# Up stage of a decoder layer: operands split in the order the products take them, bank copies with priority, norm broadcast later, two down tiles inside the last pair

## The chip, the cores and the metric

The kernel runs on one core of a Trainium2 chip, in one launch. The metric is the device time of one execution in microseconds. Three runs of the kernel before gave 1458.48, 1459.8 and 1460.78 us; the median is 1459.8 us.

## The reference

One decoder layer over 1024 positions of width 1024, in float32:

```python
h = h + hybrid_mixer(rmsnorm(h, norm_mix_g), ...)      # differential attention + conformer convolution
h = h + cross_attention(rmsnorm(h, norm_cross_g), rmsnorm(mem, norm_mem_g), w_cq, w_ckv, w_co)
h = h + conv_ffn(rmsnorm(h, norm_ffn_g), w_up, ffn_dw_w, w_down)
return rmsnorm(h, norm_final_g)

def conv_ffn(h, w_up, ffn_dw_w, w_down):
    up = jnp.einsum("bsd,df->bsf", h, w_up)            # 1024 -> 2 * 2816
    up = causal_dwconv(up, ffn_dw_w)                   # 3 taps along the sequence
    z = jax.nn.silu(up[..., :D_FF]) * up[..., D_FF:]
    return jnp.einsum("bsf,fd->bsd", z, w_down)        # 2816 -> 1024
```

The change lies in `conv_ffn`, in the last projection of the cross attention ahead of it and in the final norm behind it.

## The kernel before

Arrays stand with channels on the 128 partitions and the 1024 positions along the free dimension. A float32 product is made from three passes (`mm3`, lines 198 to 200): each operand is split into a rounded high part and the low rest, and hi*lo, lo*hi and hi*hi are added up in one PSUM bank of 128x512. A split (`split`) is a cast on ScalarE (line 220) and a subtraction on VectorE (line 221); weights of the other stages are split in `split_w` (lines 181 and 182).

The stages that matter here follow one another on TensorE.

*co*: the output projection of the cross attention, eight tiles `m`, each one `proj` of 48 matmuls into a two-bank tile `BIG`. For each half of a tile VectorE adds the residual to the bank (line 1220), the residual coming by a DMA that ScalarE's queue issues (line 1219) into a half-width buffer; ScalarE squares the sum for the norm (line 253), and VectorE adds the square to `acc` (line 254); ScalarE scales by the norm's gain into `x_` (line 1222); SyncE stores the whole tile to `h2_dr` (line 1223).

*up*: 22 pairs `p_` of a gate tile and a value tile. Both rows of weights, both halves of the 1024 input channels and both halves of the positions make a 2x2 by 2x2 block product, done with seven block products instead of eight (`product`, four k-tiles of three passes, 12 matmuls each). The weight operands are a11, a12, a22 and the sums q1 to q4 (`w_unit`; the sums are made by GpSimd, line 1191); the input operands are b11, b21, b22 and the differences n1, n2, t3, t4 (`unit`, in `late_sums` and in the loop over `m`). A pair runs as `prod1` (a11 with b11 into bank `b`; `b` copied out as p1, line 1291; a12 with b21 into bank `a`), `prod2` (q2 with n2 added to `b`; `b` copied as u2, line 1307; q3 with t3 into bank `c`; q1 with n1 added to `b`; `b` copied as u4, line 1312) and `prod3` (q4 with b22 added to `b`, a22 with t4 added to `c`). The three copies are on ScalarE and go into half-width buffers; the next product into `b` waits for them. After that come the taps of the depthwise convolution (line 1318 on ScalarE, line 1320 on VectorE), Silu on ScalarE (line 1331), and sums and products on VectorE (lines 1328, 1332, 1333, 1335); the result goes to `z_dr` (line 1336). The pair's order on TensorE is: `prod2(p)`, `prod1(p+1)`, `prod3(p)`; `prod1(0)` and `prod1(1)` come first. The inverse root mean square is found by `rf_stats` between them (16 small matmuls on line 1261, then a power on GpSimd, line 231) and spread over the partitions by `rf_bcast` (line 245) ahead of `prod2(0)`.

*down*: `z` is loaded back and split (`z_load`), the weights `dn` are split, and `down(c)` takes two of the 22 tiles at a time: for each of eight output tiles 12 matmuls into a `BIG`, which VectorE adds to the residual `h2` (line 1394). The last four tiles are in `final()`, with the norm and the output.

What sets the order: TensorE's order around the change is written out by hand (`tc.manual_schedule`). The order of the other queues (ScalarE, VectorE, GpSimd, SyncE) is fixed when the program is built, by a planner (`schedule_with_timeline_sim=True`, line 1559) that goes by readiness on its own estimate of time, and among ready instructions by priority; priority is the place in the program, and `tc.high_priority(offset=150)` puts an instruction 150 places forward. On the chip each queue is worked through in that fixed order.

Buffers that matter: 26 full-width buffers `t` (`R()`, `T()`), which hold the operands of the *co* stage (16 of them until its end) and then 26 of the input operands; 8 buffers `q` (`Q()`); 5 buffers `t2` (`T2()`) for the tiles of *co* and for weights and weight sums; 2 `whi` and 2 `wlo`, which `WU()` uses for weights by turns with `t2`; 3 buffers `raw`; 5 half-width buffers `half` (`halfT()`); eight PSUM banks `ub` (`UB()`) in *up*, which are the same banks as `BIG` and the others in *co* and *down*.

Of the kernel before, what the change touches and what calls it, by code (L numbers as in the profile page):

```python
# [10 lines left out]
F32R = mybir.dt.float32r  # L11
# [46 lines left out]
def hybrid_block_kernel(ctx: ExitStack, tc: tile.TileContext, xT, memT, pos, vecs, lams, ropec,  # L58
# [24 lines left out]
    def Q(dt=F32):  # L83
        return pq.tile([P, S], dt, tag="q", name=nm("q"))
# [16 lines left out]
    def halfT(dt=F32):  # L101
        return sm_.tile([P, HALF], dt, tag="half", name=nm("half"), bufs=5)
# [30 lines left out]
    def vcol(name, i=0):  # L133
        o, w = _COLS[name]
        return vec[:, o + i:o + i + 1]
# [66 lines left out]
    def hs(h):  # L202
        return slice(h * HALF, (h + 1) * HALF)
# [814 lines left out]
    def T2(dt=F32):  # L1018
        return p2.tile([P, S], dt, tag="t2", name=nm("t2"))
# [128 lines left out]
    late = []  # L1148

    def late_sums(j):  # L1150

        lo_, hi_ = xg[j], xg[4 + j]
        xb["b22"][j] = unit(hi_[:, hs(1)])
        nc.vector.scalar_tensor_tensor(out=lo_[:, hs(0)], in0=lo_[:, hs(0)], scalar=-1.0, in1=hi_[:, hs(1)],
                                       op0=ALU.mult, op1=ALU.subtract)
        xb["n2"][j] = unit(lo_[:, hs(0)])
        nc.vector.tensor_tensor(out=lo_[:, hs(1)], in0=hi_[:, hs(1)], in1=lo_[:, hs(1)], op=ALU.subtract)
        xb["t3"][j] = unit(lo_[:, hs(1)])
        nc.vector.scalar_tensor_tensor(out=hi_[:, hs(0)], in0=lo_[:, hs(0)], scalar=-1.0, in1=hi_[:, hs(0)],
                                       op0=ALU.mult, op1=ALU.subtract)  # L1160

    raws, wts, pairs = {}, {}, {}

    def w_load(p_):
# [10 lines left out]
    def WU():  # L1175

        tag = ("t2", "t2", "whi", "wlo", "t2", "whi", "wlo")[wcount[0] % 7]
        wcount[0] += 1
        return T2(F32R) if tag == "t2" else pw[0].tile([P, S], F32R, tag=tag, name=nm("wu"), bufs=2)

    def w_unit(name, p_):
        if p_ >= FT:
            return
        a, b = raws[p_]
        pr = pairs.setdefault(p_, {})

# [24 lines left out]
        wts[(name, p_)] = u  # L1211

    for m in range(8):
        ps = proj(need("co", m), xs_co) if m > 1 else co[m]
        hh = T2()
        x_ = Q()
        for half in range(2):
            res = halfT()
            nc.scalar.dma_start(out=res, in_=h_dr[m][:, hs(half)])
            nc.vector.tensor_tensor(out=hh[:, hs(half)], in0=ps[:, hs(half)], in1=res, op=ALU.add)  # L1220
            square_into(acc, hh[:, hs(half)], m == 0, hs(half))
            nc.scalar.mul(x_[:, hs(half)], hh[:, hs(half)], vcol("g_ffn", m))
        nc.sync.dma_start(out=h2_dr[m], in_=hh)
        xg.append(x_)
        if m == 6:
            w_load(0)
            for name in ("a11", "a12"):
                w_unit(name, 0)
        j = m % 4
        xb["b11" if m < 4 else "b21"][j] = unit(x_[:, hs(0)])  # L1230
        if m < 4:
            nc.vector.tensor_tensor(out=x_[:, hs(0)], in0=x_[:, hs(0)], in1=x_[:, hs(1)], op=ALU.subtract)
# [46 lines left out]
    def ev():  # L1279
        return halfT()  # L1280

    st = {}

    def prod1(p_):
        if p_ >= FT:
            return
        d = st[p_] = {}
        d["b"], d["a"] = UB(), UB()
        product(d["b"], "a11", p_, "b11", True)
        d["p1"] = ev()  # L1290
        nc.scalar.copy(out=d["p1"], in_=d["b"])
        product(d["a"], "a12", p_, "b21", True)

    def out1(p_):
# [8 lines left out]
    def prod2(p_):  # L1303
        d = st[p_]
        product(d["b"], "q2", p_, "n2", False)
        d["u2"] = ev()
        nc.scalar.copy(out=d["u2"], in_=d["b"])  # L1307
        d["c"] = UB()
        product(d["c"], "q3", p_, "t3", True)
        product(d["b"], "q1", p_, "n1", False)  # L1310
        d["u4"] = ev()
        nc.scalar.copy(out=d["u4"], in_=d["b"])
        d["uv"] = Q()
        nc.vector.tensor_tensor(out=d["uv"][:, hs(1)], in0=d["c"], in1=d["u4"], op=ALU.add)

# [22 lines left out]
    w_load(1)  # L1338
    with tc.manual_schedule(engines={mybir.EngineType.PE}):
        for name in ("a11", "a12"):  # L1340
            w_unit(name, 1)
        prod1(0)
        rf = rf_stats()
        for name in ("q2", "q3", "q1"):
            w_unit(name, 0)
        prod1(1)
        rf_bcast(rf)
        out1(0)
        for p_ in range(FT):
            w_unit("q4", p_)  # L1350
            w_unit("a22", p_)
            w_load(p_ + 2)
            prod2(p_)
            if p_ > 0:
                w_unit("a11", p_ + 1)
                w_unit("a12", p_ + 1)
                prod1(p_ + 1)
            out1(p_ + 1)
            for name in ("q2", "q3", "q1"):
                w_unit(name, p_ + 1)  # L1360
            prod3(p_)
    u_scope.close()


    big[0] = ctx.enter_context(tc.tile_pool(name="big2", bufs=2, space=PSUM, reuse_waits="tile"))
    bank[0] = ctx.enter_context(tc.tile_pool(name="bank3", bufs=4, space=PSUM, reuse_waits="tile"))
    wend[0] = len(seq)
    h2 = []
    for m in range(8):
        h2.append(Q())  # L1370
        nc.sync.dma_start(out=h2[m], in_=h2_dr[m])
    zt = {}
    zpos = [0]

# [6 lines left out]
            zt[zpos[0]] = (hi, lo)  # L1381
            zpos[0] += 1

    def down(c):
        ws = [need("dn", c, 1), need("dn", c + 1, 2)]
        z_load(c + 3)
        zs = [zt.pop(c), zt.pop(c + 1)]
        for m in range(8):
            ps = BIG()
            for i in range(2):  # L1390
                for h in range(2):
                    mm3(ps[:, hs(h)], (ws[i][0][:, bs(m)], ws[i][1][:, bs(m)]),
                        (zs[i][0][:, hs(h)], zs[i][1][:, hs(h)]), i == 0, i == 1)
            nc.vector.tensor_tensor(out=h2[m], in0=h2[m], in1=ps, op=ALU.add)  # L1394

    def final():
# [16 lines left out]
        def write(sl, rb):  # L1413
            w = sl.stop - sl.start
            g = S // w
            for m0 in range(0, 8, g):
                o = T()
# [19 lines left out]
        for m in range(8):  # L1437
            evac(m, banks[m], sl)

        gf = T()  # L1440
        nc.sync.dma_start(out=gf, in_=gfin.unsqueeze(0).to_broadcast([P, D]))
        hT = {}

        def residual(tb):
            hT[tb] = T()
# [12 lines left out]
            return ps  # L1458

        def finish(tb, ps):  # L1460
            h_, o = hT.pop(tb), T()
            ss = small(2, "fs", 2)
            for c in range(2):
                nc.vector.tensor_tensor(out=h_[:, hs(c)], in0=h_[:, hs(c)], in1=ps[c], op=ALU.add)
# [26 lines left out]
                residual(tb + 1)  # L1491
            finish(tb, ps)

    z_load(1)
    for c in range(0, FIN[0], 2):
        down(c)
    z_load(FT - 1)
    final()

# [63 lines left out]
```

## Time and profile before

| | |
|---|---|
| median of three runs | 1459.8 us |
| the profiled execution's own time | 1461.06 us |
| its span, first to last instruction | 1459.3 us |
| mean granted clock of TensorE | 0.988 of full speed |
| busy share of the span: TensorE, VectorE, ScalarE, GpSimd | 96%, 70%, 39%, 13% |
| *up*, from the last matmul of *co* to the first of *down* | 736.3 to 1194.2 us |

The span is what the profiler saw between the first and the last instruction; the execution's own time is 1.8 us longer, and 1.3 us above the median. A matmul of 512 columns is shown with 0.39 us, but in an unbroken row the next starts 0.23 us later: the starts tell the pace. "idle before <-releaser" names what ended the idle time of an engine ahead of an instruction.

### The profile page before, as it was taken

What the parts mean: (1) busy time and instruction counts of PE and PEld (TensorE: products, weight loads), DVE (VectorE), ACT (ScalarE), POOL (GpSimd) and SP (SyncE); (2) the same over time, 40 slices, a digit from 0 to 9 for tenths busy, and PEclk for the clock granted to TensorE, in tenths of its full rate; (3) what the DMA queues carried; (4) which work ended last, traced back from release to release, by engine and by line L of the source; (5) the groups of instructions that cost most, each with busy time, mean ns of one, the idle gap of its engine ahead of it and who ended that gap; (6) DMA issues with size and microseconds to landing.
All of it is one profiled execution on the core that took longest, in us unless ns stands there. A gap on an engine that the chain in (4) does not pass through costs nothing.

```text
span 1459.3 us, 17309 instructions
## 1 busy us (share of the span) xinstructions
PE 1407.3 (96%) x6709; PEld 1155.2 (79%) x6709; DVE 1026.5 (70%) x1375; ACT 573.3 (39%) x1015; POOL 193.7 (13%) x169
## 2 busy tenths in 40 slices
PE   9999999999999999999979999999999989999997
PEld 6888887777777888888867778778877867888886
DVE  7899998878855424454676787778787896666546
ACT  6211224677763323344453444434444451211103
POOL 0000000013110000000043322333332300000001
PEclk9999999999999999999989999999999999999999
DMA  6132225523405421103421222222222284323003
GB/s 225 40 94 65 70 82 148 175 85 87 116 15 194 166 80 58 58 30 115 137 87 57 73 87 73 76 83 87 73 87 73 85 326 166 105 69 101 15 1 116
DMA packets 44131, 141.54 MB, mean 97 GB/s; under 512 B 5776, under 2 KB 8080, under 8 KB 44048
## 3 DMA queue, kind: packets, MB, share of 16 engines
q1 hardware_dynamic: 37552, 123.65, 25.9%
q10 hardware_dynamic: 6496, 16.78, 3.6%
q8 instruction: 53, 0.87, 0.2%
q14 instruction: 30, 0.25, 0.1%
HBM read 101.51 MB, written 28.41 MB: 89 GB/s over the span
## 4 chain that ended last, share of the span: by engine, by line
PE 76%; DVE 9%; ACT 4%; issue 4%; DMA 4%; POOL 2%; SPq 0%; POOLq 0%; ACTq 0%; DVEq 0%
PE big L198 15%; PE big L199 15%; PE big L200 15%; PE ub L198 5%; PE ub L199 5%; PE ub L200 5%; DVE q L1320 2%; POOL t L1191 2%; PE big L703 2%; PE tb L772 2%; PE big L701 2%; DMA uraw<-in_wu_dram 2%; ACT q L1318 2%; PE bk L198 1%; PE bk L199 1%
## 5 line engine op out<-in xcount | busy, mean ns | idle before, releaser
L199 PE MATMUL big<-r,wlo 128*128 128x512 f32 x624 | 243.1, 390 | 0.6 <-DVE wlo L182 0.6
L200 PE MATMUL big<-r,whi 128*128 128x512 f32 x624 | 243.0, 389 | 0.0
L198 PE MATMUL big<-r,whi 128*128 128x512 f32 x560 | 219.1, 391 | 2.3 <-DVE r L304 1.2
L1394 DVE TENSOR_TENSOR q<-q,big 128x1024 f32<-128x1024 f32 x72 | 87.8, 1219 | 78.0 <-PE big L200 78.0
L181 ACT CAST whi<-raw 128x1024 fp32r<-128x1024 f32 x58 | 61.2, 1056 | 205.1 <-PE big L200 168.3
L1320 DVE SCALAR_TENSOR_TENSOR q<-q,vec,q 128x1023 f32<-128x1023 f32 x88 | 120.1, 1365 | 27.6 <-ACT q L1318 27.6
L199 PEld LDWEIGHTS big<-r,wlo 128*128 128x128 f32 x624 | 117.2, 188 | 24.7 <-DVE wlo L182 0.9
L200 PEld LDWEIGHTS big<-r,whi 128*128 128x128 f32 x624 | 117.2, 188 | 24.4
L198 PE MATMUL big<-r,r 128*128 128x512 f32 x320 | 126.3, 395 | 5.9 <-DVE q L1394 4.3
L198 PEld LDWEIGHTS big<-r,whi 128*128 128x128 f32 x560 | 105.1, 188 | 26.0 <-DVE r L304 2.6
L199 PE MATMUL big<-r,r 128*128 128x512 f32 x320 | 125.4, 392 | 0.0
L200 PE MATMUL big<-r,r 128*128 128x512 f32 x320 | 125.3, 392 | 0.0
L198 PE MATMUL ub<-r,wu 128*128 128x512 f32 x300 | 117.9, 393 | 6.0 <-ACT half L1307 3.1
L1191 POOL TENSOR_TENSOR t<-uraw 128x512 f32<-128x512 f32 x22 | 56.2, 2553 | 462.9 <-DMA uraw<-in_wu_dram 218.5
L200 PE MATMUL ub<-r,wu 128*128 128x512 f32 x300 | 117.2, 391 | 0.0
L199 PE MATMUL ub<-r,wu 128*128 128x512 f32 x300 | 117.2, 391 | 0.0
L198 PE MATMUL ub<-r,t 128*128 128x512 f32 x228 | 91.6, 402 | 13.5 <-ACT half L1307 8.7
L199 PE MATMUL ub<-r,t 128*128 128x512 f32 x228 | 90.2, 396 | 0.0
L200 PE MATMUL ub<-r,t 128*128 128x512 f32 x228 | 90.0, 395 | 0.0
L371 DVE SCALAR_TENSOR_TENSOR cv<-t,vec,cv 128x511 f32<-128x511 f32 (+14 forms) x120 | 83.9, 739 | 0.0
L1318 ACT ACTIVATE q<-q,vec 128x1024 f32<-128x1024 f32 x44 | 50.7, 1152 | 66.7 <-DVE q L1328 62.6
L198 PEld LDWEIGHTS big<-r,r 128*128 128x128 f32 x320 | 60.6, 189 | 20.1 <-DVE q L1394 4.8
(321 smaller groups left out, 2942.1 us busy)
## 6 DMA issues: line engine op xcount, KB each, us to landing
uraw<-in_wu_dram SPq DMA_DIRECT2D x44, 512.0 KB, 3.6
z_dr<-q SPq DMA_DIRECT2D x22, 512.0 KB, 2.6
raw<-in_wd_dram SPq DMA_DIRECT2D x22, 512.0 KB, 3.7
t<-z_dr SPq DMA_DIRECT2D x22, 512.0 KB, 4.8
raw<-in_wkv_dram SPq DMA_DIRECT2D x16, 512.0 KB, 3.6
raw<-in_wi_dram SPq DMA_DIRECT2D x14, 512.0 KB, 3.8
r<-r SPq DMA_DIRECT2D x16, 256.0 KB, 6.1
kv_dr<-r SPq DMA_DIRECT2D x8, 512.0 KB, 3.6
```

The lines of the kernel that those rows point to most:

```text
L181: nc.scalar.copy(out=hi, in_=raw)
L198: nc.tensor.matmul(out, wh, xl, start=start, stop=False, **kw)
L199: nc.tensor.matmul(out, wl, xh, start=False, stop=False, **kw)
L200: nc.tensor.matmul(out, wh, xh, start=False, stop=stop, **kw)
L371: nc.vector.scalar_tensor_tensor(out=y[:, i:], in0=x[:, :n2 - i], scalar=t, in1=y[:, i:], op0=ALU.mult, op1=ALU.add)
L701: nc.tensor.matmul(u["ps"][c][:, n0:n1], ql[rows, bs(qb)], ks[c][rows, n0:n1], start=True, stop=False)
L703: nc.tensor.matmul(u["ps"][c][:, n0:n1], qd[c][:, bs(qb)], ks[c][:, n0:n1], start=False, stop=n1 < nk)
L772: nc.tensor.matmul(av, u["at"][:, bs(j)], vsb[j // 2][:, (j % 2) * HALF + h * P:][:, :P], start=j == 0, stop=j == qb)
L1191: nc.gpsimd.tensor_tensor(out=t, in0=x, in1=y, op=ALU.add)
L1318: nc.scalar.mul(t, u, tp[2])
L1320: nc.vector.scalar_tensor_tensor(out=t[:, d:], in0=u[:, :S - d], scalar=tp[2 - d], in1=t[:, d:], op0=ALU.mult, op1=ALU.add)
L1394: nc.vector.tensor_tensor(out=h2[m], in0=h2[m], in1=ps, op=ALU.add)
```

## The change

In the *co* loop the residual half is added in place in its half-width buffer, the scaling comes ahead of the square, and each half is stored by itself; the `t2` tile is gone. n1 is no longer split in this loop. `w_unit("q2", 0)` stands right behind it. `late_sums` is replaced by loops in the order n2 (from a half-width buffer of its own), t3, n1, b22, t4. The three bank copies are in a helper `keep` with priority. `rf_bcast` and `out1(0)` go from ahead of `prod2(0)` to a place inside it, behind the q2 product and its copy. The weights q4 and a22 of the last pair are made one pair earlier, and `down_prep`, behind them, splits two weights and two tiles of `z` for *down* and loads all eight `h2`, now into `t` buffers instead of `q`. `down_first` does the output tiles 0 and 1 of `down(0)` between `prod2(21)` and `prod3(21)`, in four `ub` banks; `down(0)` starts at tile 2. In `final()` three kinds of tiles go from `t` to `q`.

```diff
@@ the co loop and the input operands
-        u = Q(F32R) if name == "a22" else WU()
+        u = Q(F32R) if name == "a22" and p_ < FT - 1 else WU()
...
+    n2 = [None] * 4
     for m in range(8):
         ps = proj(need("co", m), xs_co) if m > 1 else co[m]
-        hh = T2()
         x_ = Q()
         for half in range(2):
-            res = halfT()
-            nc.scalar.dma_start(out=res, in_=h_dr[m][:, hs(half)])
-            nc.vector.tensor_tensor(out=hh[:, hs(half)], in0=ps[:, hs(half)], in1=res, op=ALU.add)
-            square_into(acc, hh[:, hs(half)], m == 0, hs(half))
-            nc.scalar.mul(x_[:, hs(half)], hh[:, hs(half)], vcol("g_ffn", m))
-        nc.sync.dma_start(out=h2_dr[m], in_=hh)
+            hh = halfT()
+            nc.scalar.dma_start(out=hh, in_=h_dr[m][:, hs(half)])
+            nc.vector.tensor_tensor(out=hh, in0=ps[:, hs(half)], in1=hh, op=ALU.add)
+            nc.scalar.mul(x_[:, hs(half)], hh, vcol("g_ffn", m))
+            square_into(acc, hh, m == 0, hs(half))
+            nc.sync.dma_start(out=h2_dr[m][:, hs(half)], in_=hh)
...
-            xb["n1"][j] = unit(x_[:, hs(0)])
+    w_unit("q2", 0)
     for j in range(4):
-        late_sums(j)
+        n2[j] = halfT()
+        nc.vector.scalar_tensor_tensor(out=n2[j], in0=xg[j][:, hs(0)], scalar=-1.0, in1=xg[4 + j][:, hs(1)], ...)
+        xb["n2"][j] = unit(n2[j])
+        nc.vector.scalar_tensor_tensor(out=xg[4 + j][:, hs(0)], in0=n2[j], scalar=-1.0, in1=xg[4 + j][:, hs(0)], ...)
+    for j in range(4):
+        nc.vector.tensor_tensor(out=xg[j][:, hs(1)], in0=xg[4 + j][:, hs(1)], in1=xg[j][:, hs(1)], op=ALU.subtract)
+        xb["t3"][j] = unit(xg[j][:, hs(1)])
+    for j in range(4):
+        xb["n1"][j] = unit(xg[j][:, hs(0)])
+    for j in range(4):
+        xb["b22"][j] = unit(xg[4 + j][:, hs(1)])
@@ copies and broadcast
+    def keep(d, name):
+        d[name] = halfT()
+        with tc.high_priority(offset=150):
+            nc.scalar.copy(out=d[name], in_=d["b"])
...
         product(d["b"], "q2", p_, "n2", False)
-        d["u2"] = ev()
-        nc.scalar.copy(out=d["u2"], in_=d["b"])
+        keep(d, "u2")
+        if p_ == 0:
+            rf_bcast(rf)
+            out1(0)
@@ the end of up
+    def down_prep():
+        wend[0] = len(seq)
+        need_("dn", 0)
+        z_load(0)
+        need_("dn", 1)
+        z_load(1)
+        for m in range(8):
+            h2.append(T())
+            nc.sync.dma_start(out=h2[m], in_=h2_dr[m])
...
+    def down_first():
+        ws = [prepped[("dn", c)] for c in range(2)]
+        for m in range(2):
+            for h in range(2):
+                b = UB()
+                for i in range(2):
+                    mm3(b, (ws[i][0][:, bs(m)], ws[i][1][:, bs(m)]), (zt[i][0][:, hs(h)], zt[i][1][:, hs(h)]), i == 0, i == 1)
+                nc.vector.tensor_tensor(out=h2[m][:, hs(h)], in0=h2[m][:, hs(h)], in1=b, op=ALU.add)
...
             prod2(p_)
+            if p_ == FT - 1:
+                down_first()
...
+            if p_ == FT - 2:
+                w_unit("q4", p_ + 1)
+                w_unit("a22", p_ + 1)
+                down_prep()
             prod3(p_)
...
-        for m in range(8):
+        for m in range(first, 8):
```

## Rows read from the trace of the kernel before

**Rows 1.** The page: busy time of the engines, share of the span, instructions.
```profile
PE 1407.3 (96%) x6709; PEld 1155.2 (79%) x6709; DVE 1026.5 (70%) x1375; ACT 573.3 (39%) x1015; POOL 193.7 (13%) x169
```
**Rows 2.** Stretches: length, busy us by engine, granted clock, DMA share, GB/s.
```profile
777.80:1166.90 389.10, 377.37 (x1652) 309.10 (x1652) 307.96 (x354) 172.95 (x258) 128.09 (x76) 1.00 0.23 79
1166.90:1194.40 27.50, 24.56 (x103) 19.89 (x101) 24.77 (x26) 17.55 (x20) 0.00 (x0) 0.94 0.84 303
1194.40:1211.00 16.60, 10.68 (x37) 8.02 (x36) 13.74 (x13) 3.88 (x4) 0.00 (x0) 0.79 1.02 402
1211.00:1426.50 215.50, 215.50 (x953) 177.99 (x952) 126.53 (x112) 33.46 (x37) 0.00 (x0) 1.00 0.20 64
```
**Rows 3.** TensorE's order of time, start of up: start, us, instruction, idle before, releaser.
```profile
736.32 0.39 PE L200 MATMUL big<-r,whi 128*128 128x512 f32 x1
740.90 0.76 PE L198 MATMUL ub<-r,t 128*128 128x512 f32 x1 [4.18 <-ACT r L220]
748.80 0.40 PE L200 MATMUL ub<-r,t 128*128 128x512 f32 x1
...
756.08 0.39 PE L200 MATMUL ub<-r,wu 128*128 128x512 f32 x1
761.10 3.78 PE L245 MATMUL ub<-ident,s 128*128 128x128 f32 x16 [4.62 <-POOL s L231]
764.53 0.77 PE L198 MATMUL ub<-r,t 128*128 128x512 f32 x1
...
767.33 0.40 PE L199 MATMUL ub<-r,t 128*128 128x512 f32 x1
```
**Rows 4.** The same view, an earlier broadcast of the same size at full clock.
```profile
38.74 1.95 PE L245 MATMUL bk<-ident,s 128*128 128x128 f32 x16
```
**Rows 5.** Last co tile and its residual's load: VectorE, ScalarE and ScalarE's queue.
```profile
736.75 0.69 DVE L1220 TENSOR_TENSOR t<-big,half 128x512 f32<-128x512 f32 x1 [3.37 <-PE big L200]
...
737.48 0.33 ACTq L1219 DMA_DIRECT2D half<-h_dr  x1
738.01 0.71 ACT L1222 ACTIVATE q<-t,vec 128x512 f32<-128x512 f32 x1
740.06 0.69 DVE L1220 TENSOR_TENSOR t<-big,half 128x512 f32<-128x512 f32 x1
```
**Rows 6.** Line 1219 by itself, 440 to 460 us: its loads long ahead of use.
```profile
L1219 ACTq DMA_DIRECT2D half<-h_dr x3: 326/332/623, 445.3 to 450.8; - x3
```
**Rows 7.** GpSimd's order of time, then VectorE's splits of the same stretch.
```profile
724.04 1.29 POOL L1191 TENSOR_TENSOR t<-uraw 128x512 f32<-128x512 f32 x1 [191.43 <-DMA h_dr<-t]
747.45 6.49 POOL L1191 TENSOR_TENSOR t<-uraw 128x512 f32<-128x512 f32 x1 [10.99 <-DVE wu L221]
...
758.95 2.09 POOL L231 TENSOR_TENSOR s<-s,mhalf 128x8 f32<-128x8 f32 x1
740.67 6.10 DVE L221 TENSOR_TENSOR r<-q,r 128x512 fp32r<-128x512 f32 x10
```
**Rows 8.** Who waited for whom, 690 to 1215 us and 736 to 1211 us: us, times, longest.
```profile
PE ub L198 <- ACT half L1307: 11.7, 10, 1.5
ACT q L1331 <- DVE q L1320: 32.0, 10, 3.2
```
**Rows 9.** TensorE and VectorE in order of time, last pair and first down tiles.
```profile
1187.25 0.80 PE L198 MATMUL ub<-r,wu 128*128 128x512 f32 x1 [2.94 <-ACT half L1312]
...
1198.63 0.50 PE L198 MATMUL big<-r,r 128*128 128x512 f32 x1 [1.58 <-DVE q L1332]
...
1205.98 0.80 PE L198 MATMUL big<-r,r 128*128 128x512 f32 x1 [4.34 <-DVE q L1394]
1204.71 1.22 DVE L1394 TENSOR_TENSOR q<-q,big 128x1024 f32<-128x1024 f32 x1
```
**Rows 10.** DMA issues by line: KB each, median us from issue to landing.
```profile
half<-h_dr ACTq DMA_DIRECT2D x16, 256.0 KB, 3.0
h_dr<-t SPq DMA_DIRECT2D x8, 512.0 KB, 3.5
```

More of the change, by code (lines that the diff above doesn't have):

```diff
@@ L1146, in unit @@
         return u
[L1148 to L1160, printed above, removed]
     raws, wts, pairs = {}, {}, {}
@@ L1208, in w_unit @@
             src = wsum("qb", 1, pr["qb"][:, hs(0)], a[:, hs(1)])
-        u = Q(F32R) if name == "a22" else WU()
+        u = Q(F32R) if name == "a22" and p_ < FT - 1 else WU()
         split(src, u[:, hs(0)], u[:, hs(1)])
         wts[(name, p_)] = u
+    n2 = [None] * 4
     for m in range(8):
         ps = proj(need("co", m), xs_co) if m > 1 else co[m]
-        hh = T2()
         x_ = Q()
         for half in range(2):
-            res = halfT()
-            nc.scalar.dma_start(out=res, in_=h_dr[m][:, hs(half)])
-            nc.vector.tensor_tensor(out=hh[:, hs(half)], in0=ps[:, hs(half)], in1=res, op=ALU.add)
-            square_into(acc, hh[:, hs(half)], m == 0, hs(half))
-            nc.scalar.mul(x_[:, hs(half)], hh[:, hs(half)], vcol("g_ffn", m))
-        nc.sync.dma_start(out=h2_dr[m], in_=hh)
+            hh = halfT()
[4 more added lines that the diff above has]
+            nc.sync.dma_start(out=h2_dr[m][:, hs(half)], in_=hh)
         xg.append(x_)
+        j = m % 4
+        xb["b11" if m < 4 else "b21"][j] = unit(x_[:, hs(0)])
+        if m < 4:
+            nc.vector.tensor_tensor(out=x_[:, hs(0)], in0=x_[:, hs(0)], in1=x_[:, hs(1)], op=ALU.subtract)
         if m == 6:
@@ L1228, in hybrid_block_kernel @@
                 w_unit(name, 0)
[L1229 to L1232, printed above, removed]
-            xb["n1"][j] = unit(x_[:, hs(0)])
-    for j in range(4):
-        late_sums(j)
+    w_unit("q2", 0)
+    for j in range(4):
+        n2[j] = halfT()
+        nc.vector.scalar_tensor_tensor(out=n2[j], in0=xg[j][:, hs(0)], scalar=-1.0, in1=xg[4 + j][:, hs(1)],
+                                       op0=ALU.mult, op1=ALU.subtract)
+        xb["n2"][j] = unit(n2[j])
+        nc.vector.scalar_tensor_tensor(out=xg[4 + j][:, hs(0)], in0=n2[j], scalar=-1.0, in1=xg[4 + j][:, hs(0)],
+                                       op0=ALU.mult, op1=ALU.subtract)
+    for j in range(4):
[5 more added lines that the diff above has]
+        xb["b22"][j] = unit(xg[4 + j][:, hs(1)])
     for j in range(4):
@@ L1289, in prod1 @@
         product(d["b"], "a11", p_, "b11", True)
-        d["p1"] = ev()
-        nc.scalar.copy(out=d["p1"], in_=d["b"])
+        keep(d, "p1")
         product(d["a"], "a12", p_, "b21", True)
@@ L1310, in prod2 @@
         product(d["b"], "q1", p_, "n1", False)
-        d["u4"] = ev()
-        nc.scalar.copy(out=d["u4"], in_=d["b"])
+        keep(d, "u4")
         d["uv"] = Q()
@@ L1336, in prod3 @@
         nc.sync.dma_start(out=z_dr[p_], in_=tg)
[L1338 to L1367, printed above, removed]
     h2 = []
-    for m in range(8):
-        h2.append(Q())
-        nc.sync.dma_start(out=h2[m], in_=h2_dr[m])
     zt = {}
@@ L1382, in z_load, with need_, down @@
             zpos[0] += 1
-    def down(c):
+    def down_prep():
[7 more added lines that the diff above has]
+            nc.sync.dma_start(out=h2[m], in_=h2_dr[m])
+    def need_(kind, m):
+        load_to(index[(kind, m)])
+    def down_first():
[6 more added lines that the diff above has]
+                nc.vector.tensor_tensor(out=h2[m][:, hs(h)], in0=h2[m][:, hs(h)], in1=b, op=ALU.add)
+    w_load(1)
+    with tc.manual_schedule(engines={mybir.EngineType.PE}):
+        for name in ("a11", "a12"):
+            w_unit(name, 1)
+        prod1(0)
+        rf = rf_stats()
+        for name in ("q3", "q1"):
+            w_unit(name, 0)
+        prod1(1)
+        for p_ in range(FT):
+            if p_ < FT - 1:
+                w_unit("q4", p_)
+                w_unit("a22", p_)
+            w_load(p_ + 2)
+            prod2(p_)
+            if p_ == FT - 1:
+                down_first()
+            if p_ > 0:
+                w_unit("a11", p_ + 1)
+                w_unit("a12", p_ + 1)
+                prod1(p_ + 1)
+            out1(p_ + 1)
+            for name in ("q2", "q3", "q1"):
+                w_unit(name, p_ + 1)
+            if p_ == FT - 2:
+                w_unit("q4", p_ + 1)
+                w_unit("a22", p_ + 1)
+                down_prep()
+            prod3(p_)
+    u_scope.close()
+    big[0] = ctx.enter_context(tc.tile_pool(name="big2", bufs=2, space=PSUM, reuse_waits="tile"))
+    bank[0] = ctx.enter_context(tc.tile_pool(name="bank3", bufs=4, space=PSUM, reuse_waits="tile"))
+    def down(c, first=0):
         ws = [need("dn", c, 1), need("dn", c + 1, 2)]
@@ L1387, in down @@
         zs = [zt.pop(c), zt.pop(c + 1)]
-        for m in range(8):
+        for m in range(first, 8):
             ps = BIG()
@@ L1416, in write @@
             for m0 in range(0, 8, g):
-                o = T()
+                o = Q()
                 for i in range(g):
@@ L1438, in final @@
             evac(m, banks[m], sl)
-        gf = T()
+        gf = Q()
         nc.sync.dma_start(out=gf, in_=gfin.unsqueeze(0).to_broadcast([P, D]))
@@ L1444, in residual @@
         def residual(tb):
-            hT[tb] = T()
+            hT[tb] = Q()
             for c in range(2):
@@ L1460, in finish @@
         def finish(tb, ps):
-            h_, o = hT.pop(tb), T()
+            h_, o = hT.pop(tb), Q()
             ss = small(2, "fs", 2)
@@ L1492, in final @@
             finish(tb, ps)
-    z_load(1)
     for c in range(0, FIN[0], 2):
-        down(c)
+        down(c, 2 if c == 0 else 0)
     z_load(FT - 1)
```

2 lines of the change are left out of this document (removed).

## The prediction

> **What bounds the kernel now.** I read the page first: TensorE is busy 96% of the span, VectorE 70%, ScalarE 39% [rows 1]. A share is no speed, so I took the view of stretches next. In the down stage 953 matmuls take 215.50 us at full clock, 0.226 us each [rows 2]; that is the pace of an unbroken row, and whatever a stretch takes beyond it is loss. The same view gives a granted clock of 0.94 and 0.79 in the two stretches around the end of *up* [rows 2], so time is lost there twice, by waits and by the lower of the two clock levels behind them. Then I read TensorE in order of time where *up* begins and ends [rows 3, 9], and who ended its waits between [rows 8]. Three losses come out, and the change speaks to each:
>
> - *Start.* The last *co* matmul starts at 736.32, the first product at 740.90. At pace it would start at 736.55: 4.35 us. Its 24 matmuls then last to 749.03 (748.80 and one pace), 8.13 us instead of 5.42, since the clock fell to 1.2 GHz in the wait: 2.7 us. Behind `prod1(1)` (last start 756.08) the broadcast waits for GpSimd's power, runs 16 matmuls at half clock, and q2(0) starts at 764.53 instead of 756.31: 8.2 us, and 1.2 us more until the clock is back at 767.33 (2.80 us for seven starts) [rows 3]. Sum 7.05 and 9.4.
> - *Middle.* Ten waits for the u2 copy, 11.7 us of idle time [rows 8]. Idle is counted from modelled ends, some 0.16 us behind the pace, and the first matmul behind a wait runs longer; I put the loss at 14 us.
> - *End.* 103 matmuls in 27.50 us and 37 in 16.60 [rows 2]: 27.50 - 23.3 = 4.2 and 16.60 - 8.4 = 8.2, together 12.4 us. The first is the wait of 2.94 for u4 of pair 21, with the clock behind it; the second are the waits of 1.58 for line 1332 and of 4.34 for the first down tile's addition, and the clock [rows 9].
>
> **The change part by part.**
>
> *First product.* It starts 0.15 us after the addition of the last half tile, 740.06 + 0.69 = 740.75 [rows 5]; the cast that the row names [rows 3] makes no operand of a11 with b11. I take the addition, since the product's bank is one of that tile's. The addition waited for its residual, whose load was issued at 737.48, 0.04 us behind the first half's addition (736.75 + 0.69). Why not earlier, with five half buffers? Three loads went out long ahead [rows 6]; the fourth half buffer in the program is that of the first square. So buffers are handed out in program order, and the load of a second half has to follow the square of the first. The new program still has them in this order, and the square now comes behind the scaling, at 738.0 instead of 737.48 [rows 5]. The load goes 0.5 us later: cost 0.5. Bounds: a gain of 7.05 if the load gets free of the square, a loss of 3.5 if it must await the store of the first half [rows 10].
>
> *Order of the operands, and the broadcast later.* The first product at 741.4, two products as slow as before until 749.5, the small matmuls (1.9 us as before: 756.31 less 24 x 0.226 is 750.9, against 749.0), `prod1(1)` until 756.8, q2(0) until 759.5. n2 needs three VectorE operations for each of four tiles, t3 two: 20, with about five others, all from 741.3, when the last half tile is there. VectorE does ten such in 6.10 us [rows 7], so n2 is ready near 750 and t3 near 757, ahead of 756.8 and 762. n1, b22 and t4 are four operations each, 2.4 us, against 2.7 us of a product: they stay ahead. So the broadcast alone can hold TensorE. The power ended at 758.95 + 2.09 = 761.04, behind four sums of pair 1 (747.45 + 6.49 = 753.94, then three in 5.0, 1.7 each) [rows 7]. In the new program the sums of pair 0 no longer wait for `t2` tiles of *co*, and the first sum of pair 1 takes the buffer of a12(0), free at 749.5. Before the power is ready in the plan, two sums fit: 749.5 + 6.5 + 1.7 + 2.1 = 759.8, a wait of 0.3. I take 1.0, since GpSimd's spans are rough. The broadcast itself is 1.95 at full clock [rows 4]. So 9.4 becomes 2.95: gain 6.4. Bounds: 7.4 (no wait), and -0.7 (next but one paragraph).
>
> GpSimd's sum took 1.29 us at 724 and 6.49 us at 747, when VectorE ran its additions and subtractions without a gap [rows 7]. The Trainium skill, page "SBUF — State Buffer", section "Who interferes with whom", says that a VectorE instruction with two SBUF inputs and a GpSimd instruction that reads SBUF exclude each other for the whole instruction. By that rule the trace's 6.49 is a sum shut out by VectorE, and the denser row of splits that the change puts there speaks against it.
>
> What the rows make of that without the page: if both sums last 6.49, the power ends at 749.5 + 13.0 + 2.1 = 764.6, TensorE waits 5.1 us, and the low clock comes back with its 1.8 (3.78 instead of 1.95) and 1.2 [rows 3, 4]: 10.1 in place of 9.4. That is the lower bound and the second rival.
>
> *Copies with priority.* Priority chooses among instructions that are ready. In ten pairs ScalarE stands idle 3.2 us in front of Silu, waiting for VectorE [rows 8], and the u2 copy is queued behind Silu: ten idles, ten waits of TensorE. Had the copy been ready in the plan while ScalarE was idle, it would have got the engine. So the plan believed Silu ready first, and Silu is late on the chip because VectorE is. Priority doesn't turn such an order round. I take 0; bounds 0 and 14, and nothing below, as a copy moved forward delays only Silu, for which TensorE does not wait.
>
> *Two down tiles in the last pair.* 24 matmuls, 5.4 us, move from `down(0)` to the place of the 2.94 wait, which they cover: the 4.2 go. Behind `prod3(21)` two waits are left to judge. The two-bank tiles of *down* may still fall on the bank of c, which waits for line 1332. And VectorE worked until 1205.9 before the first tile's addition was through [rows 9], 11.5 us behind the last product; in the new program the third `BIG`, which needs the first to be added, is asked for 5.4 us behind it. Less splitting stands ahead (eight of the 26 `t` buffers now hold `h2`, so no more than four weights and four `z` are made early), and `h2` is there earlier. I put 8.2 at 3.5. Bounds: 0 and 8.2. Gain 4.2 + 4.7 = 8.9. The `h2` loads come into a stretch with a DMA share of 0.84 [rows 2] and are needed at once by two tiles only; those additions stand in four other banks, 5.4 us of `prod3(21)` cover them.
>
> *At nothing:* the q4 and a22 weights made earlier, `q` in place of `t` in `final()`, and 18 instead of 26 buffers for *down*, which has two tiles of work (21.7 us) to load and split the next; in that stage ScalarE is busy 16% and VectorE 59% [rows 2]. In *up* VectorE has 21% to spare [rows 2] for moved work.
>
> *Sum.* -0.5 + 6.4 + 0 + 8.9 = 14.8 us. The profiled execution's own time, 1461.06, becomes 1446.3. It stands 1.3 above the median of the runs, so the median after should be 1445.
>
> **The rivals.**
>
> 1. *The copies do move.* For: the ten waits are one pattern with one cause, and 150 places reach past the whole of `prod3`. Against: the idle in front of Silu, above. The 14 us go nearly whole: 13 less, 1432.
> 2. *GpSimd shut out,* as worked out above: the broadcast gains -0.7 instead of 6.4. For: 6.49 us in a row of splits [rows 7]. Against: the later sums of the same row, 1.7 each. 1445 + 7 = 1452.
> 3. *Slower: the store holds the half buffer.* The half tile now lives until its store has landed. If the load of each second half has to wait for that, a half takes 0.69 + 3.5 + 3.0 = 7.2 [rows 5, 10], a tile 14.4, against 48 x 0.226 = 10.85 on TensorE. Seven tiles lose 3.5 each, 24.7; one `BIG` in hand takes off 10.9; the last half is 3.5 later: 17. Waits of this length also cost clock (2.7 behind 4.35 [rows 3]), some 5 more: 1467. It decides from the point where store and load together pass 4.7 us. For: the load is already tied to the half before it [rows 5]. Against: five buffers, and a tile takes four.
> 4. *The end gives all back:* the bank of c and VectorE's row cost more with the clock than before, and rival 2 besides: 1458, no change.
>
> **How the numbers follow.** My forecast has 0.50, with 1440 to 1450 as its own range (the first product and the end by their nearer bounds); rival 1 0.20, rival 2 0.14, rival 3 0.08, rival 4 0.08. The range of 1431 to 1456 takes in the first three, 0.84, less some edges. This kernel can be told from no change by about 0.2%, 3 us. Faster: the first three, 0.84. Rival 4 splits into 0.06 same and 0.02 slower, with rival 3 0.10 slower.
>
> **What would show it.** The load of the last residual half some 0.5 us behind 737.5, the first product near 741.4; the broadcast's row at 1.95, not 3.78, behind q2(0), with a wait under 1.5; ten or so waits for u2 still there (rival 1: none); no wait for u4 in the last pair; behind the last product waits of 3.5 together. Wrong: waits between *co* tiles (rival 3), or GpSimd's power after 763 (rival 2).

## The result and the profile after

The changed kernel takes 1442.05 us (median of 4 runs, 1441.40 to 1445.19), the kernel before beside it 1460.29 (1458.48 to 1462.51): a ratio of 0.9879, interval 0.9859 to 0.9899. The profiled execution went from 1461.06 to 1442.12, 18.9 us less. The forecast was 1445, its sum 14.8 us. The total is close, but two of its terms are wrong in opposite directions.

In the new program line 1282 makes the three bank copies, 1206 the residual's additions, 1205 their loads, 1333 is Silu, 1419 the additions of *down*. The page's first line, in the order of [rows 1]:

```profile
PE 1399.1 (97%) x6709; PEld 1149.7 (80%) x6709; DVE 1026.7 (71%) x1377; ACT 573.5 (40%) x1015; POOL 191.7 (13%) x169
```

As many matmuls as before, in 8 us less of busy time, which I read as the low clock's share (the mean granted clock rose from 0.988 to 0.995). The rest is idle time. The start of *up*, in TensorE's order of time (answers to [rows 3]):

```profile
735.52 0.39 PE L200 MATMUL big<-r,whi 128*128 128x512 f32 x1
740.59 0.79 PE L198 MATMUL ub<-r,t 128*128 128x512 f32 x1 [4.68 <-DVE half L1206]
...
758.14 0.39 PE L200 MATMUL ub<-r,wu 128*128 128x512 f32 x1
762.40 3.64 PE L245 MATMUL ub<-ident,s 128*128 128x128 f32 x16 [3.87 <-POOL s L231]
765.80 0.48 PE L198 MATMUL ub<-r,wu 128*128 128x512 f32 x1
```

The first product starts 5.07 us behind the last *co* matmul (4.58 before), and its row now names what the forecast took for its gate, the last half tile's addition. The broadcast still waits 3.87 us for the power and still runs at the lower clock level, 3.64 us in place of 3.78. Measured as in the forecast (from the last matmul at pace to the next one at pace), its 9.4 us became 7.5. GpSimd, and VectorE behind it (answers to [rows 7]), show why:

```profile
740.01 1.27 POOL L1177 TENSOR_TENSOR t<-uraw 128x512 f32<-128x512 f32 x1 [25.20 <-DVE t L221]
741.23 1.74 POOL L1177 TENSOR_TENSOR t<-uraw,uraw 128x512 f32<-128x512 f32 x1
745.92 3.46 POOL L1177 TENSOR_TENSOR t<-t,uraw 128x512 f32<-128x512 f32 x2 [2.94 <-PE ub L200]
755.50 6.84 POOL L231 TENSOR_TENSOR s<-s,mhalf 128x8 f32<-128x8 f32 x1 [6.13 <-DVE s L229]
755.27 0.15 DVE L229 TENSOR_SCALAR s<-ub 128x8 f32<-128x8 f32 x1
755.34 5.49 DVE L221 TENSOR_TENSOR r<-q,r 128x512 fp32r<-128x512 f32 x9
760.76 0.68 DVE L1301 TENSOR_TENSOR q<-ub,half 128x512 f32<-128x512 f32 x1
```

The four sums were done by 749.4, so nothing stood ahead of the power. But this 128x8 power, 2.09 us before, lasted 6.84 us: it ran beside VectorE's row of nine splits and ended 1.5 us behind it.

Next the waits, as in [rows 8] (us, times, longest; the first row 736 to 1193 us, the others 690 to 1199):

```profile
ACT q L1333 <- DVE q L1322: 33.0, 11, 3.2
PE ub L198 <- ACT half L1282: 12.3, 11, 1.5
PE big L198 <- DVE t L1419: 0.3, 1, 0.3
```

The waits for copies are all there (the eleventh, 0.7, stood in its own row before). At the end of *up* nothing is left of the waits of [rows 9] but 0.3 us, and the clock no longer falls, as two stretches with the columns of [rows 2] show:

```profile
1180.00:1192.70 12.70, 12.70 (x58) 10.52 (x57) 11.27 (x14) 6.52 (x7) 0.00 (x0) 1.00 1.03 410
1192.70:1199.00 6.30, 5.98 (x27) 4.66 (x26) 6.30 (x7) 2.47 (x3) 0.00 (x0) 1.00 1.03 416
```

One gain stands where no step of mine looked, in `final()`. TensorE's rows there, before and after:

```profile
1432.57 0.95 PE L239 MATMUL bk<-ones,acc 128*128 128x1 f32 x8
1435.31 1.55 PE L245 MATMUL bk<-ident,s 128*128 128x128 f32 x8 [1.79 <-POOL s L231]
```

```profile
1414.65 0.95 PE L239 MATMUL bk<-ones,acc 128*128 128x1 f32 x8
1415.46 0.48 PE L198 MATMUL big<-r,r 128*128 128x512 f32 x1
...
1418.31 1.05 PE L245 MATMUL bk<-ident,s 128*128 128x128 f32 x8
```

Before, the norm's sums stood behind the last product of a block and the broadcast waited for the power. Now twelve matmuls stand between the two and cover it. That order is not in the edit: TensorE's order in `final()` is the planner's.

The account, from the start of the last *co* matmul to the start of VectorE's last instruction, is 718.40 us before and 700.52 after, 17.88 less. Loss is the time beyond 0.2267 us for each 512 columns of a matmul, added up over TensorE's rows of a stretch:

| place | forecast of the gain | loss before | loss after | gain |
|---|---|---|---|---|
| first product | -0.5 | 7.0 | 7.1 | -0.1 |
| broadcast of the norm | 6.4 | 8.5 | 6.6 | 1.9 |
| waits for copies, pairs 0 to 20 | 0 | 15.4 | 15.8 | -0.3 |
| last pair and first down tiles | 8.9 | 13.2 | 0.6 | 12.6 |
| rest of *down*, `final()` | 0 | | | 3.8, by difference |

The last *co* matmul itself is 0.8 us earlier, which makes 18.7 of 18.9.

### The profile page after: what moved, and what is told of

The parts are those of the page before. It is cut to its first block, busy times and chain, and to the rows that moved or that the text cites. A ratio compares the mean times of both kernels' runs of the same rounds, so it can differ in the third digit from the quotient of the medians.

```text
span 1440.2 us, 17346 instructions
## 1 busy us (share of the span) xinstructions
PE 1399.1 (97%) x6709; PEld 1149.7 (80%) x6709; DVE 1026.7 (71%) x1377; ACT 573.5 (40%) x1015; POOL 191.7 (13%) x169
## 4 chain that ended last, share of the span: by engine, by line
PE 79%; DVE 9%; ACT 4%; issue 3%; DMA 3%; POOL 2%; SPq 0%; POOLq 0%; ACTq 0%; DVEq 0%
PE big L198 16%; PE big L199 15%; PE big L200 15%; PE ub L198 5%; PE ub L199 5%; PE ub L200 5%; DVE q L1322 2%; PE big L703 2%; PE tb L772 2%; PE big L701 2%; POOL t L1177 2%; ACT q L1320 2%; DMA uraw<-in_wu_dram 1%; PE bk L198 1%; PE bk L200 1%
## 5 line engine op out<-in xcount | busy, mean ns | idle before, releaser
L1419 DVE TENSOR_TENSOR t<-t,big 128x1024 f32<-128x1024 f32 x70 | 85.2, 1218 | 62.0 <-PE big L200 61.9
L198 PE MATMUL big<-r,r 128*128 128x512 f32 x312 | 121.7, 390 | 0.3 <-DVE t L1419 0.3
L199 PE MATMUL big<-r,r 128*128 128x512 f32 x312 | 121.5, 389 | 0.0
L200 PE MATMUL big<-r,r 128*128 128x512 f32 x312 | 121.5, 389 | 0.0
L1177 POOL TENSOR_TENSOR t<-uraw 128x512 f32<-128x512 f32 x22 | 50.1, 2276 | 460.7 <-DMA uraw<-in_wu_dram 424.2
L181 ACT CAST r<-raw 128x1024 fp32r<-128x1024 f32 x22 | 23.0, 1051 | 135.2 <-PE big L198 134.5
```

The costliest lines, as they stand in the source:

```text
L181: nc.scalar.copy(out=hi, in_=raw)
L198: nc.tensor.matmul(out, wh, xl, start=start, stop=False, **kw)
L199: nc.tensor.matmul(out, wl, xh, start=False, stop=False, **kw)
L200: nc.tensor.matmul(out, wh, xh, start=False, stop=stop, **kw)
```

## The experiments

All are edits of the changed kernel, except the second. Times are medians beside runs of the kernel before. Where a few us matter I also give the time of that account, "from *co* to the end", since it leaves out the stages ahead of the change. There executions differ: the last *co* matmul stood between 734.4 and 736.3 in most profiles, but at 738.7 and 738.8 in two, whose granted clock behind a wait for a DMA near 240 us was 0.66 and 0.74 from 242 to 250 us, against 1.00 in the change (and 0.83 in the profile of before, which may be the 0.8 us above).

**The priority of the copies**

```
     d[name] = halfT()
-    with tc.high_priority(offset=150):
-        nc.scalar.copy(out=d[name], in_=d["b"])
+    nc.scalar.copy(out=d[name], in_=d["b"])
```

> The changed kernel with the three bank copies at ordinary priority. Theory (priority chooses only among instructions that are ready, and these copies had no ready rival): the copies stand where they stood, the same ten waits of TensorE for the u2 copy, 1442 us, within 2. Rival (priority gave part of the gain): the copies stand later in some pairs, more or longer waits, up to 14 us slower, about 1450.

1442.37 us (1441.43 to 1443.44). The same eleven waits, 12.2 us in place of 12.3, and on all five engines the same instructions in the same order. Priority is worth nothing here. Its profile also gives the noise of one program: from *co* to the end 701.59 against 700.52, and the broadcast waited 4.46 in place of 3.87, so that its stretch lost 8.5 us, as much as in the kernel before. Differences of 1 us in that account mean nothing, and the 1.9 gained at the broadcast are not clear of noise either.

**The end part alone**, put into the kernel before (edit: `down_prep`, `down_first`, q4 and a22 of pair 21 a pair earlier, `h2` in `t`, the outputs in `q`, as in the diff of the change)

> The kernel before with the end part of the change alone: weights, z and h2 of the first down tiles asked for in pair 20, two down tiles inside pair 21, h2 in the t buffers and the outputs in q. Theory: the loss at the end of up goes from 13.2 us to under 1 and the tail loses another 3 us, together 15.7: 1460.3 - 15.7 = 1444.6. Rival 1 (the tail's 3 us came with the start): 1447.7. Rival 2 (my forecast's size for the end, 8.9): 1451.

1443.60 us (1441.77 to 1443.88), ratio 0.9882 (0.9868 to 0.9897); from *co* to the end 701.93. Of the 17.88 us, 16.5 come from the end part alone. The start of *up* is as slow as before:

```profile
760.11 3.78 PE L245 MATMUL ub<-ident,s 128*128 128x128 f32 x16 [4.70 <-POOL s L231]
```

So all that was done to operands, broadcast and copies is worth about 1.4 us, hardly more than the noise.

**The end without its tiles**

```
-            if p_ == FT - 1:
-                down_first()
...
-        down(c, 2 if c == 0 else 0)
+        down(c)
```

> The changed kernel without the two tiles in pair 21 (the first weights, z and h2 are still asked for in pair 20; down does all eight tiles). Theory as forecast: the tiles cover only the wait for u4 of pair 21 (4.2 us with the clock behind it) and one more tile's time behind the last product, so 4 to 6 us are lost, about 1447. Rival A (the tiles are everything, the early loads nothing): the whole 12.6 us come back, 1454.6. Rival B (the early loads are everything): 1442, no change.

1443.56 us (1441.87 to 1445.56); 701.74. The tiles that gave the change its name are worth 1.2 us, hardly more than the noise. Without them the last pair has one wait of 0.94 for a copy, and the wait of 2.94 for u4 [rows 9] doesn't come back. The term of 4.2 us in my sum, tiles covering that wait, was wrong: the wait was gone anyway. Rival B came closest. So the end part had to be taken apart.

**The three other thirds**: only the weights of pair 21 made early; only the down operands asked for early; neither, so that just the buffers of `h2` and of the outputs differ from before (all without tiles):

```
# weights of 21 only            # loads only                  # buffers only
-    down_prep()                -    w_unit("q4", p_ + 1)     -    w_unit("q4", p_ + 1)
+    (h2, z as before,          -    w_unit("a22", p_ + 1)    -    w_unit("a22", p_ + 1)
+     behind up)                     down_prep()              -    down_prep()  (as before, behind up)
```

> The end part taken apart, first third: the changed kernel without the two tiles in pair 21, and with h2, z and the down weights asked for behind up as before; only q4 and a22 of pair 21 are still made a pair earlier, and h2 stands in the t buffers. Without the tiles alone the loss at the end was 2.0 us, so the tiles are not what took 13.2 to 0.6. Theory X (the last pair was late because VectorE's row held its weights behind other splits; making them early is the gain): about 1443.5. Theory Y (the gain is in asking for the down operands early): the waits of 1.6 and 4.3 us behind the last product are back with the clock, 1451 to 1455.

> Second third: no tiles in pair 21, q4 and a22 of pair 21 in their old place; h2, z and the first down weights asked for in pair 20 as in the changed kernel. Theory X (the weights of pair 21): the wait for u4 of pair 21 is back, 3 us of wait and the clock, 1448 or more. Theory Y (the operands of down): 1443.5.

> Last third: no tiles, no early weights, no early loads; all that is left of the end part is that h2 stands in eight of the 26 t buffers and the outputs in q. Theory Z (with fewer t buffers free, VectorE is handed fewer splits of down weights ahead of the taps and the first additions, and that alone cuts its late row): 1444 to 1448. Theories X and Y: all of the 12.6 us are back, 1455.

Weights only 1446.70 (1445.60 to 1447.39), loads only 1443.46 (1442.95 to 1444.41), buffers only 1447.14 (1446.20 to 1448.44); from *co* to the end 704.68, 702.08 and 706.04. Theory X falls: with and without early weights the times agree (1446.7 and 1447.1; 1443.6 and 1443.5), and what differs from *co* to the end (1.4 and 0.3) is near the noise. Y holds for 4.0 us (706.04 - 702.08). Z holds for the bulk: with nothing but other buffers at the end, 718.4 less the 1.4 of the start (taken as the difference of the second experiment) becomes 706.0, 11 us. Of these, 7 lie around the last pair, where the loss of 13.2 becomes 6.3, and 3.7 in `final()`. This is VectorE in the last pair, first of the kernel before, then of the kernel with only the buffers changed:

```profile
1182.35 1.22 DVE L182 TENSOR_TENSOR r<-raw,r 128x1024 fp32r<-128x1024 f32 x1 [0.30 <-ACT r L181]
...
1185.29 1.22 DVE L182 TENSOR_TENSOR r<-raw,r 128x1024 fp32r<-128x1024 f32 x1
...
1187.62 1.22 DVE L221 TENSOR_TENSOR r<-t,r 128x1024 fp32r<-128x1024 f32 x1
...
1190.48 1.22 DVE L221 TENSOR_TENSOR r<-t,r 128x1024 fp32r<-128x1024 f32 x1
1191.62 2.35 DVE L182 TENSOR_TENSOR r<-raw,r 128x1024 fp32r<-128x1024 f32 x2
1193.89 1.22 DVE L221 TENSOR_TENSOR r<-t,r 128x1024 fp32r<-128x1024 f32 x1
...
1195.63 1.21 DVE L221 TENSOR_TENSOR r<-t,r 128x1024 fp32r<-128x1024 f32 x1
1196.76 1.22 DVE L182 TENSOR_TENSOR r<-raw,r 128x1024 fp32r<-128x1024 f32 x1
1197.90 0.68 DVE L1332 TENSOR_TENSOR q<-ub,half 128x512 f32<-128x512 f32 x1
```

```profile
1176.82 2.35 DVE L221 TENSOR_TENSOR r<-t,r 128x1024 fp32r<-128x1024 f32 x2
1179.09 1.22 DVE L182 TENSOR_TENSOR r<-raw,r 128x1024 fp32r<-128x1024 f32 x1
...
1182.02 1.22 DVE L182 TENSOR_TENSOR r<-raw,r 128x1024 fp32r<-128x1024 f32 x1
...
1184.95 1.22 DVE L1337 TENSOR_TENSOR q<-q,q 128x1024 f32<-128x1024 f32 x1
1186.09 0.68 DVE L1330 TENSOR_TENSOR q<-ub,acc 128x512 f32<-128x512 f32 x1
1188.13 0.69 DVE L1334 TENSOR_TENSOR q<-ub,half 128x512 f32<-128x512 f32 x1 [1.36 <-PE ub L200]
1188.74 1.28 DVE L1322 SCALAR_TENSOR_TENSOR q<-q,vec,q 128x1023 f32<-128x1023 f32 x1
```

Lines 182 and 221 on 128x1024 tiles are splits of down weights and of z, some 1.14 us each in a row. The kernel before does nine of them between the additions at 1332 of the last two pairs (1177.85 and 1197.90), eight from 1185.3 on, and TensorE's next bank waits for the second addition. With only the buffers changed four stand between the two (line 1334 there, 1173.89 and 1188.13), none behind 1183.2, and the addition finds VectorE waiting for TensorE (1.36). The loads of `h2` go out earlier too (from 1163.2 us, before from 1198.4), but that is not where the gain lies: the first additions of *down* still hold TensorE for 1.13, 0.42 and 2.71 us, in place of 4.34. That buffers do it is shown; that it is the `t` buffers given to `h2`, which are then not free for early splits, is my reading, since the outputs' move to `q` was not tried by itself. The planner's better order in `final()` stands in this kernel too (sums at 1419.86, broadcast at 1423.52 without a wait), so that gain also comes with the buffers.

**The broadcast two products later**

```
-        if p_ == 0:
-            rf_bcast(rf)
-            out1(0)
         d["c"] = UB()
...
         keep(d, "u4")
+        if p_ == 0:
+            rf_bcast(rf)
+            out1(0)
```

> The changed kernel with the norm's broadcast of pair 0 two products later again (behind q1 in place of q2: 24 matmuls, 5.4 us). Theory: TensorE no longer waits for GpSimd's power (3.87 us of wait; the power ended at 762.3), the broadcast runs at full clock (1.95 instead of 3.64): 6.56 us of loss become about 2, so 1437.5. Rival (the time comes back as a wait of pair 0's last products for the bank that the broadcast's result must first drain, or for operands n1 and t3 that are later than q2's): 1440 to 1442.

1438.32 us (1437.51 to 1442.06), ratio 0.9854 (0.9836 to 0.9872); 696.75, 3.8 less than the change. It is the theory's time, and the row is at full clock and without a wait:

```profile
764.59 1.95 PE L245 MATMUL ub<-ident,s 128*128 128x128 f32 x16
```

The rival's way of giving time back is there too: counted from the last *co* matmul the kernel is 5.9 us ahead of the change at 777 us, but only 2.0 behind a wait of 3.41 for a u2 copy at 818.94 (0.94 in the change) and the low clock that follows it.

**The power left out** (this norm's power on GpSimd; VectorE multiplies in its place, all other work is the same)

```
-        return rstd(ps[:, :NB], NB, D)
+        t = small(NB)
+        nc.vector.tensor_scalar(out=t, in0=ps[:, :NB], scalar1=1.0 / D, scalar2=EPS, op0=ALU.mult, op1=ALU.add)
+        r = small(NB)
+        nc.vector.tensor_tensor(out=r, in0=t, in1=mhalf[:, :NB], op=ALU.mult)
+        return r
```

> The changed kernel with the power of this one norm left out: VectorE multiplies by a constant behind its own line 229 (so the factors are wrong, all other work the same). Theory (GpSimd's 6.84 us for this 128x8 power is the delay, and the line 229 at 755.27 is already in time): the broadcast is ready by 756, no wait behind q2(0), 5.5 us less, 1436.5. Rival (the place of line 229 in VectorE's order is the delay too): VectorE's line comes later or the broadcast still waits over 1 us, 1439 to 1442.

1443.49 us (1440.02 to 1446.04), and 699.85 from *co* to the end, so no gain that shows, but the question is answered in the rows:

```profile
755.10 0.15 DVE L1262 TENSOR_SCALAR s<-ub 128x8 f32<-128x8 f32 x1
...
758.18 0.16 DVE L1264 TENSOR_TENSOR s<-s,mhalf 128x8 f32<-128x8 f32 x1
```

```profile
758.39 2.05 PE L245 MATMUL ub<-ident,s 128*128 128x128 f32 x16
...
781.28 0.50 PE L198 MATMUL ub<-r,wu 128*128 128x512 f32 x1 [3.51 <-ACT half L1286]
```

With VectorE's line as late as ever (755.10), the broadcast waits for nothing: GpSimd's 6.84 us were the delay. Of the 5.5 us so won, counted from the last *co* matmul, only 0.6 are left behind the next wait for a u2 copy, 3.51 us with the low clock behind it.

**Silu behind the next pair's u2 copy**

```
-        nc.scalar.activation(tg, tg, AF.Silu)
...
+        def silu():      # Silu, the product with tv, the store of z
+        ...
         keep(d, "u2")
+        if gate:
+            with tc.issue_after(last_copy[0].ins):
+                gate.pop()()
```

> The changed kernel with Silu of pair p (and the product with it and the store of z) put behind the u2 copy of pair p+1 in ScalarE's order; pair 21 as it was. Theory (the ten waits of TensorE come from the copy's place behind a Silu that waits for VectorE): no wait of TensorE for the u2 copy, 14.6 us of loss become under 3, 1429. Rival A (VectorE sets the pace of a pair, the wait only moves to the next bank or tile): 1440 to 1444. Rival B (z and its buffers are now held longer, so the taps or the last pair's loads come late): slower than 1444.

1433.39 us (1431.64 to 1434.24), ratio 0.9816 (0.9803 to 0.9829); 692.89, 7.6 less. This profile's broadcast cost 1.8 us more than that of the change, so the copies gave some 9. Of the waits for copies, which the change left at 12.3 us, this is left:

```profile
PE ub L198 <- ACT half L1282: 5.3, 6, 1.8
```

The cause of [rows 8] is shown: the copy stood behind a Silu that waited for VectorE, and only an order written out moves it. The theory wanted 3 us less; five waits of 0.2 to 1.8 in late pairs stay, so rival A keeps a part.

**Both halves of the residual first**

```
+        hhs = [halfT(), halfT()]
         for half in range(2):
-            hh = halfT()
-            nc.scalar.dma_start(out=hh, in_=h_dr[m][:, hs(half)])
+            nc.scalar.dma_start(out=hhs[half], in_=h_dr[m][:, hs(half)])
+        for half in range(2):
+            hh = hhs[half]
             nc.vector.tensor_tensor(out=hh, in0=ps[:, hs(half)], in1=hh, op=ALU.add)
```

> The changed kernel with both half buffers of a co tile's residual taken before the tile's squares (the same five buffers, the same work). Theory (the load of the second half waits for the square of the first, by the order in which buffers are handed out): the last half's load is issued long ahead of 736, the first product starts near 737.2 instead of 740.59 and at full clock, 3.3 + 2.7 us less: 1436. Rival (the buffer is then held by the store of an earlier half instead, 3.5 us): the load stays near 736.5 or goes later, 1442 or slower.

1440.72 us (1435.36 to 1446.63), not to be told from the change; 701.74. The first product came as the theory said, 1.77 us behind the last *co* matmul (at 738.80 here) in place of 5.07, and the gain was lost eight us later:

```profile
740.57 0.50 PE L198 MATMUL ub<-r,t 128*128 128x512 f32 x1 [1.38 <-DVE half L1208]
...
748.74 0.80 PE L198 MATMUL ub<-r,t 128*128 128x512 f32 x1 [3.13 <-DVE r L221]
```

```profile
742.84 0.68 DVE L1225 SCALAR_TENSOR_TENSOR half<-q,q 128x512 f32<-128x512 f32 x1
...
747.41 0.68 DVE L1225 SCALAR_TENSOR_TENSOR half<-q,q 128x512 f32<-128x512 f32 x1
748.01 0.68 DVE L221 TENSOR_TENSOR r<-q,r 128x512 fp32r<-128x512 f32 x1
```

The second product needs the split of the last b21; in VectorE's order it stands behind n2's sums (line 1225). The long first wait had hidden that. The load of the second half was issued at 731.23, 7.6 us ahead of the last *co* matmul, so the order in which the half buffers are taken does hold it back, as the forecast read; the store of the half tile (rival 3) holds nothing here.

**Together**: the broadcast and Silu edits, then these with the residual first and with n2's sums put behind that split (`tc.issue_after` on the last split of b21)

> The changed kernel with the broadcast behind q1 and Silu behind the next pair's u2 copy, the two edits that each won alone (4.1 and 9 us). Theory (they work on different waits and add up): 1442.3 - 4.1 - 9 = 1429, and below both kernels. Rival (GpSimd's row of weights, which wait for their loads, sets the pace once TensorE is ahead, and the later wait takes part of it): 1432 to 1434, no better than Silu's move alone.

> The changed kernel with the broadcast behind q1, Silu behind the next pair's u2 copy, both half buffers of a residual taken first, and VectorE's n2 sums put behind the split of the last half tile that the second product reads. Read from the last co matmul to the last matmul of the program, since the stages before that differ by up to 4 us between executions of one kernel. There the changed kernel took 697.6 us, broadcast and Silu together 685.4, the residual alone 698.8: its first product came 3.3 us sooner, but the second then waited 3.1 us for that split, which stood behind n2 in VectorE's order. Theory (the order took that gain): with the split first, the wait and its low clock go, 5 to 6 us less than 685.4, about 680, and 1424 to 1428 us in all. Rival (VectorE is simply full there, and another operand is late in place of that one): 684 to 688, 1429 to 1433.

Two edits: 1432.83 us (1428.25 to 1433.38), no better than Silu alone by its median. But its profile is one of the two with a late *co* (738.66), and from *co* to the end it took 688.35, 4.5 less than Silu alone: in this account they add up. All of them: 1427.86 us (1427.21 to 1430.36), ratio 0.9782 (0.9768 to 0.9796), which beats both kernels, the change by 14 us. From *co* to the end it is 686.27, 2.1 less than the two, where the theory wanted over 5 (683.4 by the count of the expectation, which stops at the last matmul: between theory and rival). The wait for the split is gone, and a copy behind ScalarE's row of casts is late next, with the power after it:

```profile
758.09 0.50 PE L198 MATMUL ub<-r,wu 128*128 128x512 f32 x1 [1.77 <-ACT half L1288]
...
764.34 2.05 PE L247 MATMUL ub<-ident,s 128*128 128x128 f32 x16 [1.65 <-POOL s L233]
```

## Why the prediction was right or wrong

**First product, -0.5.** It starts 0.49 us later against the last *co* matmul: the size is right. The way there is half wrong. The load was issued 1.25 us behind that matmul (736.77), as before (1.16), ahead of the scaling and the square; in ScalarE's queue it stands behind two casts that had waited 4.94 us for TensorE. It was its addition that came 3.1 us after the issue in place of 2.6.

```profile
735.72 1.14 ACT L220 CAST wu<-t 128x512 fp32r<-128x512 f32 x2 [4.94 <-PE big L199]
736.77 0.33 ACTq L1205 DMA_DIRECT2D half<-h_dr  x1
```

**Broadcast, 6.4 us forecast, 1.9 measured.** The step that failed is the wait that I put at 1.0 us ahead of the broadcast; it was 3.87, with the low clock behind it. I let the sums of pair 1 run late and be followed by a power of 2.1 us. In fact the sums were early and the power itself took 6.84. This is rival 2's mechanism on another instruction, at a price between forecast and rival. The Trainium skill, page "SBUF — State Buffer", section "Who interferes with whom", says that a VectorE instruction with two SBUF inputs contends with a GpSimd instruction that reads SBUF. The 6.84 us beside nine such splits agree with that; but the 2.09 of [rows 7] had such splits beside it too, so that rule of the Trainium skill alone does not tell the two apart. I had weighed it for the sums alone.

**Copies, 0.** Right in size and in cause, and shown twice: without priority the order is the same, and with Silu moved by hand most of the waits go (12.3 us become 5.3).

**End, 8.9 us forecast, 12.6 measured.** The mechanism that I named in half a sentence (eight of the `t` buffers hold `h2`, so fewer splits stand ahead) fits the rows where most of the gain lies; I priced it inside 4.7 and gave the tiles 4.2. Taken apart, of the 12.6 the buffers give some 7, the early operands 4.0, the tiles 1.2, and the early weights of pair 21 nothing clear of the noise.

**`final()`, at nothing.** About 3.8 us. "`q` in place of `t`" looked like a change of names, but with only the buffers changed the planner's order is another.

The errors (-4.5 for the broadcast, +3.7 and +3.8 for end and tail) leave 3.0 us, which is why 1445 stood so close to 1442. So close a hit is luck: the wrong prices offset each other in part.

## What to carry to other kernels

Where a planner orders the work, buffers decide how far it runs ahead: moving `h2` and the tiles of `final()` between pools was worth more here than every other part of the change. A wait that is removed uncovers the next one, so read who is late second before pricing it; twice here a wait of 3 to 4 us came back as another within 25 us. And 150 places of priority moved nothing here, while an order written out did.

## What the hardware showed

How long the 128x8 power lasts went with VectorE's row beside it. Here are the power and VectorE's first instruction behind its row of splits, in the kernel with the residual first and in the last kernel:

```profile
757.63 9.85 POOL L231 TENSOR_TENSOR s<-s,mhalf 128x8 f32<-128x8 f32 x1 [3.72 <-DVE s L229]
765.90 0.68 DVE L1303 TENSOR_TENSOR q<-ub,half 128x512 f32<-128x512 f32 x1
```

```profile
752.62 11.66 POOL L233 TENSOR_TENSOR s<-s,mhalf 128x8 f32<-128x8 f32 x1 [6.12 <-DVE s L231]
762.70 0.68 DVE L1308 TENSOR_TENSOR q<-ub,half 128x512 f32<-128x512 f32 x1
```

In the change and in all of its edits that have this power, eleven profiles, it ended 1.58 to 1.60 us after VectorE started its first instruction with one operand in PSUM (765.90, 762.70, 760.76 and so on), however many splits stood ahead: 6.84, 9.85 and 11.66 us for the same work. But splits beside it do not always keep a GpSimd instruction out, nor does its size decide. In the change, GpSimd's larger sums did get between VectorE's instructions (some 1.74 each near 746, with single VectorE instructions stretched from 0.68 to about 1.76). In the kernel before, the first sum was kept for 6.49 us, and the power, directly behind the last sum, took 2.09 although splits ran beside it from 758.38 to 761.95. What lets the one in and not the other, no run here tells.
